# Seven-product down projection, paced between the gate and up products, in a SwiGLU encoder layer on one Trainium2 core

## The chip, the core and the metric

One NeuronCore of a Trainium2 chip runs the whole layer. Its engines work side by side, each through its own instruction queue in order: PE (TensorE, matrix products into PSUM), DVE (VectorE), ACT (ScalarE), POOL (GpSimd) and SP (SyncE, which here issues the loads and stores). The metric is the device time of one execution in microseconds (us), taken over several runs; less is better.

## What is computed

The layer works on 512 tokens of width 1024, in float32:

```
x  = LN1(alpha*x + 0.5*(silu(x@wg1) * (x@wu1)) @ wd1)      # FFN 1, wg/wu 1024x2816, wd 2816x1024
h  = x @ w_in ; sparse top-k attention (8 heads) and a gated short convolution on parts of h
x  = LN2(alpha*x + concat(attention, conv) @ w_out)
x  = LN3(alpha*x + 0.5*(silu(x@wg2) * (x@wu2)) @ wd2)      # FFN 2, same shapes
x  = x + sigmoid(x @ ple_gate_w) * (p @ ple_proj_w)
```

## The kernel before, in words

**Exactness.** Every float32 operand is kept as two tiles of TensorE's rounded format, `hi` and `lo` (their sum is the number), and every product is three matmuls: hi·hi, lo·hi and hi·lo in the order of `PASSES` (line 59). `split` (lines 110 to 112) makes the two: ACT casts `hi` (L111), DVE subtracts to get `lo` (L112). Tiles live in pages of 4 KB a partition, given out in a ring by `page` and `free` (lines 86 to 94); 38 of them.

**FFN.** `ffn` (from line 244) is called for both FFNs. The 2816 hidden columns are 22 chunks of 128. Chunks 0 and 1 are done by `plain` (L256 to L274). The others go in pairs by `two` (L309 to L352): a pair's gate and up products, 1024 x 256 weights against 1024 x 512 activations, are cut into quarters and done by seven products in place of eight (`prod`, L319). A product is 24 matmuls of 128x256 into a PSUM bank. ACT or DVE adds the seven results up in SBUF (L340 to L349): one ACT copy and seven DVE additions a pair. `weights` (L276 to L307) makes a pair's weight operands: per matrix four DVE sums and differences (L293, L294, L299, L300) and splits. `put_chunk` (L332) makes silu(gate)*up, and `put` splits it (L111, L112 with `hf`).

**Down projection.** The chunks are taken in groups of 4, 4, 4, 4 and 6 (`GROUPS1`, `GROUPS2`). After a group's chunks the down projection adds them to the output rows `nat`: for each half of the 1024 output columns and each of the four blocks of 128 tokens, every chunk's three 128x512 matmuls (L132) into one bank, and one DVE operation that scales and adds the bank to `nat` (L406). That is 2 x 4 x 4 x 3 = 96 matmuls and 8 of these additions for a group of four. `wd_rows` (L368) loads the weights 512 KB at a time and splits each (four for a group of four). The last group of six is also done so, with the layer norm behind it (L382 to L396).

**Order.** A scheduler puts the instructions on the engines by their place in the program, moved forward by the offsets of `tc.high_priority`; nothing else paces the operand work against PE.

Of the kernel before, what the change touches and what calls it, by code (L numbers as in the profile page):

```python
# [29 lines left out]
NPAGES = 38  # L30
WSTEPS = (1, 2, 1)
# [5 lines left out]
AHEAD_D2 = 0  # L37
NEMB = 2
# [25 lines left out]
def layer_kernel(ctx: ExitStack, tc: tile.TileContext, x, ln1_g, ln1_b, ffn1_wg, ffn1_wu, ffn1_wd, w_in,  # L64
# [3 lines left out]
    pp = ctx.enter_context(tc.tile_pool(name="pp", bufs=1, space=bass.MemoryType.PSUM))  # L68

# [22 lines left out]
    def free(*tiles):  # L92
        for t in tiles:
# [3 lines left out]
              "fill": BANKS[0], "qk": BANKS[1], "av": BANKS[2], "pt": BANKS[3]}  # L97
# [146 lines left out]
    def ffn(X, wg, wu, wd, ln_g, ln_b, first, load_nat, groups, nplain, ahead, ahead_f, ahead_d):  # L244
# [11 lines left out]
        def plain(fc, ws, cuts, ah):  # L256
# [13 lines left out]
            hf = ring("hf", 2, [P, 512])  # L270
            s_t = ring("a", 2, [P, 512])
            nc.scalar.activation(s_t, ps["g"], AF.Silu)
            nc.vector.tensor_mul(hf, s_t, ps["u"])
            return put(hf)  # L274

        def weights(w, fc, ops, pages):  # L276
# [8 lines left out]
            ops["A11"] = a11[:, 0], a11[:, 1]  # L285
            yield
            a2 = page([P, 4, 2 * P]), page([P, 4, 2 * P])
            split(*a2, r[1])
            ops["A12"], ops["A22"] = (tuple(z[:, :, m * P:(m + 1) * P] for z in a2) for m in range(2))
# [7 lines left out]
            ops["S1"], ops["S2"] = (tuple(z[:, i] for z in h12) for i in range(2))  # L297
            yield
            nc.vector.tensor_sub(S3, A11, A21)  # L299
            nc.vector.tensor_sub(S4, A12, S2)  # L300
            free(*r, s12)
# [4 lines left out]
            pages += [a11, *a2, *h12, *h34]  # L306
            yield  # L307

        def two(fc, ah):  # L309

            W, pages = {nm: {} for nm, _ in mats}, []
            steps = [weights(w, fc, W[nm], pages) for nm, w in mats]
            with tc.high_priority(offset=ah):
                for n in WSTEPS:
                    for g in steps:
                        for _ in range(n):
                            next(g)

            def prod(a, b):  # L319

                ps = bank("all").rearrange("p (m n) -> p m n", m=2)
                for i, (nm, _) in enumerate(mats):
                    mm(ps[:, i], [((W[nm][a][0][:, c], W[nm][a][1][:, c]), (X.q[b][0][:, c], X.q[b][1][:, c])) for c in range(4)])
                return ps


            e = [page([P, 2, 2, 256], F32) for _ in range(2)]
            k = [page([P, 2, 2, 256], F32) for _ in range(2)]
            p1, u2, u3, u4 = k[0][:, 0], k[0][:, 1], k[1][:, 0], k[1][:, 1]
            h = []  # L330

            def put_chunk(m):  # L332
                hf = ring("hf", 2, [P, 512])
                h3 = hf.rearrange("p (a b) -> p a b", a=2)
                s_t = ring("a", 2, [P, 2, 256])
                nc.scalar.activation(s_t, e[m][:, :, 0], AF.Silu)  # L336
                nc.vector.tensor_mul(h3, s_t, e[m][:, :, 1])  # L337
                h.append(put(hf))
# [4 lines left out]
            p5 = prod("S1", "T1")  # L343
            nc.vector.tensor_add(u4, p5, u2)
            nc.vector.tensor_add(e[0][:, 1], prod("S4", "B22"), u4)  # L345
            put_chunk(0)
            nc.vector.tensor_add(u3, prod("S3", "T3"), u2)
            nc.vector.tensor_add(e[1][:, 1], p5, u3)
            nc.vector.tensor_add(e[1][:, 0], prod("A22", "T4"), u3)  # L349
            put_chunk(1)  # L350
            free(*pages, *e, *k)
            return h  # L352

        f0 = 0
        for gi, per in enumerate(groups):
            last = gi == len(groups) - 1
            h = []
            while len(h) < per:
                fc = f0 + len(h)
                if fc < nplain:  # L360
                    h.append(plain(fc, first if fc == 0 else {}, 2, ahead))
                    if len(h) == nplain:
                        free(*X.q["B12"])
                        X.sums()
                else:
                    h += two(fc, ahead if fc < 4 else ahead_f)
            wds, held = {}, {}

            def wd_rows(i, half):
                if (i, half) not in wds:  # L370
                    n2 = min(2, per - i)
                    u = unit(rows(wd[:, half * 512:(half + 1) * 512], (f0 + i) * P, n2), [P, n2, 512], ahead_d)
                    for k in range(n2):
                        wds[i + k, half] = (u[0][:, k], u[1][:, k])
                        held[i + k, half] = u if k == n2 - 1 else ()
                return wds[i, half]

            if gi == 0 and load_nat:
                load_nat()
            if last:  # L380
                X.done()
                g_t, b_t = bcast(ln_g[0]), bcast(ln_b[0])  # L382
                yT = new_xT()
                for t in range(NTB):
                    for half in range(2):
                        acc = bank("all")
                        for i in range(per):
                            mm(acc, [(both(h[i], ts(t)), wd_rows(i, half))], first=i == 0, last=i == per - 1)
                            if t == NTB - 1:
                                free(*held[i, half])  # L390
                        dst = nat[t][:, half * 512:(half + 1) * 512]
                        nc.vector.scalar_tensor_tensor(dst, acc, CY, dst, op0=ALU.mult, op1=ALU.add)  # L392
                        nc.vector.bn_stats(stats[t][:, half], dst)
                    ln_tb(nat[t], stats[t], g_t, b_t)
                    transpose_tb(yT, t, "all")
            else:  # L396
                for half in range(2):
                    acc = [bank("all") for _ in range(NTB)]
                    for i in range(per):
                        wv = wd_rows(i, half)  # L400
                        for t in range(NTB):
                            mm(acc[t], [(both(h[i], ts(t)), wv)], first=i == 0, last=i == per - 1)
                        free(*held[i, half])
                    for t in range(NTB):
                        dst = nat[t][:, half * 512:(half + 1) * 512]
                        nc.vector.scalar_tensor_tensor(dst, acc[t], CY, dst, op0=ALU.mult, op1=ALU.add)  # L406
            free(*h)
            f0 += per
# [14 lines left out]
    def embed(t):  # L423

        prj.append(page([P, 1024], F32))
        for half in range(2):
            hs = slice(half * 512, (half + 1) * 512)
            ps = bank("fill" if t < NEMB else "all")
            mm(ps, [((p_T[0][:, c, ts(t)], p_T[1][:, c, ts(t)]),
                     (wp[c][0][:, 0, hs], wp[c][1][:, 0, hs])) for c in range(2)])  # L430
            nc.scalar.copy(prj[t][:, hs], ps)  # L431
            yield
# [3 lines left out]
    warm = sb.tile([P, 512], F32, name="warm")  # L436
# [110 lines left out]
    dm = sb.tile([P, 1280], F32, name="dm")  # L547
    for t in range(NTB):
        w_ = (t + 1) * P
        d = dm[:, TOFF[t]:TOFF[t + 1]]  # L550
# [4 lines left out]
    nc.vector.memset(dm[0:64, 64:128], -BIG)  # L555
# [18 lines left out]
    def choose():  # L574
# [105 lines left out]
    def softmax(h):  # L680
# [3 lines left out]
        a = soft[h] = ring("a", 2, [P, 1280])  # L684
        st = ring("ss", 2, [P, NTB, 3])
        for t in range(NTB):
            w_ = (t + 1) * P
            o = slice(TOFF[t], TOFF[t + 1])
            ps = bank("qk")
            mm64(ps[:, :w_], qT[j], e, ts(t), kT[j][:, e, :w_], kL[j][:, e, :w_])  # L690
            nc.vector.tensor_tensor_reduce(a[:, o], ps[:, :w_], dm[:, o], -slope, 3.0e38, ALU.add, ALU.min, st[:, t, 0:1])
            nc.scalar.activation(a[:, o], a[:, o], AF.Exp, bias=st[:, t, 0:1], scale=-1.0, accum_out=st[:, t, 1:2])
            nc.vector.reciprocal(st[:, t, 2:3], st[:, t, 1:2])
            nc.vector.tensor_scalar(a[:, o], a[:, o], st[:, t, 2:3], None, op0=ALU.mult)

# [46 lines left out]
    free(*v)  # L742
# [30 lines left out]
    for t in range(NTB):  # L773
# [39 lines left out]
```

## Time and profile before

| | |
|---|---|
| runs of the kernel before | 1024.43, 1026.31, 1027.77 us (median 1026.31) |
| the profiled execution | 1025.2 us, of which the span of its trace is 1023.2 us |
| busy over the span | PE 98%, DVE 80%, ACT 43%, POOL 2% |
| HBM traffic | 101 GB/s over the span |

The trace gives each instruction's engine, source line, tiles and time. The span runs from the first to the last instruction. A matmul's busy time is modelled and overlaps the next one's, so the pace of a stretch of matmuls is read from the starts of neighbouring stretches.

### The profile page before, as it was taken

How to read it: one execution, taken by the hardware profiler on the slowest of the kernel's cores; microseconds unless marked ns; L12 is line 12 of the kernel's file. 1: busy time of each engine (PE TensorE's matmuls, PEld its weight loads, DVE VectorE, ACT ScalarE, POOL GpSimd, SP SyncE). 2: the span in 40 equal slices, each digit the busy share in tenths (PEclk: the TensorE clock that was granted, in tenths of full speed). 3: DMA queues.
4: the chain of work that ended last, by engine and by line, in shares of the span. 5: the costliest groups of instructions: out<-in, count | busy, mean ns of one | idle time of the engine just before them, and what ended most of it. 6: DMA issues, size and time to landing. Idle time of an engine off the chain costs nothing.

```text
span 1023.2 us, 15533 instructions
## 1 busy us (share of the span) xinstructions
PE 1004.2 (98%) x6311; PEld 901.9 (88%) x6311; DVE 823.5 (80%) x1289; ACT 443.2 (43%) x627; POOL 25.0 (2%) x35
## 2 busy tenths in 40 slices
PE   8999999999999999999999999999999999999998
PEld 7989999898998878888878778989999898998887
DVE  7997868978697958999479988896868969689952
ACT  7444334433355235332586836543425325246221
POOL 1000000000000200000000011000000000000100
PEclk9999999999999999999999999999999999999999
DMA  9532324323245231514012222331324322227111
GB/s 303 159 114 81 107 83 145 94 80 115 83 138 183 62 95 36 143 37 124 21 53 92 83 76 90 131 117 47 119 84 145 102 80 88 82 90 260 53 41 51
DMA packets 99606, 104.57 MB, mean 102 GB/s; under 512 B 5968, under 2 KB 82000, under 8 KB 99536
## 3 DMA queue, kind: packets, MB, share of 16 engines
q1 hardware_dynamic: 99536, 103.60, 32.2%
q8 instruction: 49, 0.80, 0.3%
q14 instruction: 21, 0.17, 0.1%
HBM read 101.49 MB, written 2.10 MB: 101 GB/s over the span
## 4 chain that ended last, share of the span: by engine, by line
PE 89%; DMA 4%; DVE 3%; ACT 3%; SPq 1%; issue 1%; POOLq 0%; ACTq 0%; DVEq 0%
PE bk L132 85%; ACT pg L111 2%; DVE pg L112 1%; PE bk L522 1%; DMA pg<-in_ffn_wu_dram 1%; DMA pg<-in_w_in_dram 1%; PE bk L523 1%; PE bk L720 1%; DMA pg<-in_x_t_dram 1%; DMA pg<-in_ple_proj_w_dram 1%; DMA pg<-in_ffn_wd_dram 0%; SPq L214 0%; PE bk L146 0%; DMA pg<-in_ple_gate_w_dram 0%; PE bk L708 0%
## 5 line engine op out<-in xcount | busy, mean ns | idle before, releaser
L132 PE MATMUL bk<-pg,pg 128*128 128x256 f32 (+1 forms) x2832 | 496.0, 333 | 5.7 <-DVE nat L755 2.2
L132 PEld LDWEIGHTS bk<-pg,pg 128*128 128x128 f32 x2832 | 427.3, 190 | 57.4 <-ACT pg L111 3.1
L111 ACT CAST pg<-pg 128x1024 fp32r<-128x1024 f32 (+1 forms) x270 | 260.4, 976 | 309.9 <-PE bk L132 76.2
L112 DVE TENSOR_TENSOR pg<-pg,pg 128x1024 fp32r<-128x1024 f32 (+1 forms) x270 | 301.6, 1128 | 42.5 <-ACT pg L111 35.8
L132 PE MATMUL bk<-xq,pg 128*128 128x256 f32 x2208 | 274.4, 283 | 2.5 <-DVE mv L158 1.5
L132 PEld LDWEIGHTS bk<-xq,pg 128*128 128x128 f32 x2208 | 269.1, 192 | 6.5 <-ACT pg L431 1.9
L132 PE MATMUL bk<-xT,pg 128*128 128x512 f32 (+2 forms) x600 | 133.1, 381 | 0.3 <-ACT xT L111 0.2
L132 PEld LDWEIGHTS bk<-xT,pg 128*128 128x128 f32 (+1 forms) x600 | 109.9, 186 | 21.5 <-ACT xT L111 0.5
L132 PE MATMUL bk<-pg,xT 128*128 128x512 f32 (+1 forms) x312 | 69.5, 374 | 1.3 <-DVE nat L392 1.3
L132 PEld LDWEIGHTS bk<-pg,xT 128*128 128x128 f32 x312 | 55.0, 188 | 11.4 <-ACT pg L111 1.7
L336 ACT ACTIVATE a<-pg 128x512 f32<-128x512 f32 x40 | 25.2, 631 | 70.3 <-DVE pg L345 63.6
L111 ACT CAST pg<-hf 128x512 fp32r<-128x512 f32 (+1 forms) x56 | 34.6, 619 | 38.6 <-DVE hf L337 20.8
L112 DVE TENSOR_TENSOR pg<-hf,pg 128x512 fp32r<-128x512 f32 (+1 forms) x56 | 38.4, 685 | 4.3 <-ACT pg L111 4.0
L406 DVE SCALAR_TENSOR_TENSOR nat<-bk,nat 128x512 f32<-128x512 f32 x64 | 40.4, 683 | 0.5 <-PE bk L132 0.2
L337 DVE TENSOR_TENSOR hf<-a,pg 128x512 f32<-128x512 f32 x40 | 27.5, 688 | 14.5 <-ACT a L336 14.5
L345 DVE TENSOR_TENSOR pg<-bk,pg 128x512 f32<-128x512 f32 x20 | 13.8, 691 | 27.8 <-PE bk L132 27.5
L160 POOL TENSOR_TENSOR mv<-mv,mhalf 128x1 f32<-128x1 f32 x12 | 17.8, 1481 | 628.0 <-DVE mv L159 628.0
L293 DVE TENSOR_TENSOR pg<-pg,pg 128x512 f32<-128x512 f32 x40 | 27.2, 686 | 5.9 <-DMA pg<-in_ffn_wg_dram 5.9
L299 DVE TENSOR_TENSOR pg<-pg 128x512 f32<-128x512 f32 x40 | 27.5, 686 | 3.0 <-PE bk L132 3.0
L112 DVE TENSOR_TENSOR pg<-bk,pg 128x512 fp32r<-128x512 f32 (+2 forms) x37 | 22.5, 627 | 8.5 <-ACT pg L111 8.1
L294 DVE TENSOR_TENSOR pg<-pg,pg 128x512 f32<-128x512 f32 x40 | 27.3, 684 | 0.0
L300 DVE TENSOR_TENSOR pg<-pg,pg 128x512 f32<-128x512 f32 x40 | 27.1, 685 | 0.1
(100 smaller groups left out, 613.8 us busy)
## 6 DMA issues: line engine op xcount, KB each, us to landing
pg<-in_ffn_wd_dram SPq DMA_DIRECT2D x44, 512.0 KB, 4.0
pg<-in_ffn_wu_dram SPq DMA_DIRECT2D x43, 512.0 KB, 4.7
pg<-in_ffn_wg_dram SPq DMA_DIRECT2D x43, 512.0 KB, 3.9
pg<-in_w_in_dram SPq DMA_DIRECT2D x28, 512.0 KB, 3.6
pg<-in_w_out_dram SPq DMA_DIRECT2D x8, 512.0 KB, 3.9
pg<-in_ple_gate_w_dram SPq DMA_DIRECT2D x8, 512.0 KB, 5.1
pg<-in_x_t_dram SPq DMA_DIRECT2D x8, 256.0 KB, 5.9
nat<-in_x_dram SPq DMA_DIRECT2D x4, 512.0 KB, 9.2
```

Of the source, the lines that this page charges most:

```text
L111: nc.scalar.copy(hi, src)
L112: nc.vector.tensor_sub(lo, src, hi.bitcast(F32))
L132: nc.tensor.matmul(ps, lhsT=st[a], rhs=mv[b], start=first and i == 0 and k == 0, stop=last and i == n - 1 and k == 2)
L160: nc.gpsimd.tensor_tensor(mv[:, 3:4], mv[:, 2:3], mhalf, op=ALU.pow)
L293: nc.vector.tensor_add(S1, A21, A22)
L294: nc.vector.tensor_sub(S2, S1, A11)
L299: nc.vector.tensor_sub(S3, A11, A21)
L300: nc.vector.tensor_sub(S4, A12, S2)
L336: nc.scalar.activation(s_t, e[m][:, :, 0], AF.Silu)
L337: nc.vector.tensor_mul(h3, s_t, e[m][:, :, 1])
L345: nc.vector.tensor_add(e[0][:, 1], prod("S4", "B22"), u4)
L406: nc.vector.scalar_tensor_tensor(dst, acc[t], CY, dst, op0=ALU.mult, op1=ALU.add)
```

## The change

In both FFNs the down projection of the first four groups is done by the same seven-product scheme as the pairs. A group of four chunks is two pairs; token halves, the two chunks of a pair and the two halves of the output columns are the quarters. A product is 12 matmuls of 128x512: two banks (token blocks), two pairs, three passes. The results are not added up in SBUF: a bank holds a running sum of products, and after a product DVE adds the bank to each part of `nat` that contains that sum.

The products' operands: `pair_ops` makes the hidden side (one split of 768 columns, four DVE sums of 256, one split of 1024 a pair). `Down.prep` makes the weight side: four DVE differences (L305), and for each of the seven operands `parts`: ACT writes minus the rounded weight into `lo` (L299), a DMA issued by POOL adds the weight to `lo` in SBUF (L300), ACT casts `hi` (L301). The seven splits' DVE subtraction is thus not there.

The pairs' own products add up in PSUM in the same way, with four ACT copies and three DVE additions a pair. Their banks are four, the down projection's the other four. One list, `order`, fixes which product follows which: from the third product of the next pair on, two down products after three pair products. Loads and operand work stand in the program at a set planned time ahead of their product. Chunks 0 and 1 and the last group of six stay as they were.

There are 41 pages now. The embedding product `prj` goes to DRAM after it is made and is loaded again at the end; the attention's `dm` and softmax rows are in pages.

```diff
-NPAGES = 38
-WSTEPS = (1, 2, 1)
+NPAGES = 41
+LEAD_L, LEAD_S, LEAD_DL, LEAD_DS = 16.0, 8.0, 18.0, 13.0
+T_PLAIN, T_PAIR, T_DOWN = 11.5, 2.9, 2.7
...
+        def pair_ops(pair):
+            A12, A22, A11, A21 = (pair[:, i] for i in range(4))
+            a = page([P, 4, 256]), page([P, 4, 256])
+            split(a[0][:, :3], a[1][:, :3], pair[:, :3])
+            s_ = page([P, 4, 256], F32)
+            nc.vector.tensor_add(s_[:, 0], A21, A22)
...
+            split(*sums, s_)
...
+            def parts(self, name):
+                src = self.raw[name]
+                hi, lo = self.w[name] = page([P, 2, 512]), page([P, 2, 512])
+                nc.scalar.mul(lo, src, -1.0)
+                nc.gpsimd.dma_start(lo, src, accum_op=ALU.add)
+                nc.scalar.copy(hi, src)
...
+            def product(self, banks, a, w, first, *outs):
+                w = self.w.pop(w)
+                for b in range(2):
+                    for i, (q, sums) in enumerate(self.pairs):
+                        st = sums if a[0] == "S" else q
+                        for n, (x_, y_) in enumerate(PASSES):
+                            nc.tensor.matmul(banks[b], lhsT=st[x_][:, SLOT[a], ts(b)], rhs=w[y_][:, i],
+                                             start=first and i == 0 and n == 0, stop=i == 1 and n == 2,
+                                             skip_group_check=not first)
+                free(*w)
+                for m, n in outs:
+                    for b in range(2):
+                        dst = nat[2 * m + b][:, n * 512:(n + 1) * 512]
+                        nc.vector.scalar_tensor_tensor(dst, banks[b], CY, dst, op0=ALU.mult, op1=ALU.add)
+            def products(self):
+                two_banks = lambda: [bank("down") for _ in range(2)]
+                x_, y_ = two_banks(), two_banks()
+                self.product(x_, "A11", "B11", True, (0, 0))
+                yield
+                self.product(y_, "S1", "T1", True, (1, 1))
+                yield
+                self.product(x_, "S2", "T2", False, (0, 1))
+                yield
+                self.product(x_, "S3", "T3", False, (1, 1))
+                yield
+                self.product(y_, "S4", "B22", False, (0, 1))
...
+                self.product(x_, "A22", "T4", False, (1, 0))
+                yield
+                self.product(two_banks(), "A12", "B21", True, (0, 0))
...
-            nc.scalar.copy(p1, prod("A11", "B11"))
-            nc.vector.tensor_add(e[0][:, 0], prod("A12", "B21"), p1)
-            nc.vector.tensor_add(u2, prod("S2", "T2"), p1)
...
+                nc.scalar.copy(e[0][:, 0], product(x_, "A11", "B11", True))
+                yield
+                nc.scalar.copy(e[1][:, 1], product(y_, "S1", "T1", True))
+                yield
+                nc.scalar.copy(e[0][:, 1], product(x_, "S2", "T2", False))
+                yield
+                nc.vector.tensor_add(e[0][:, 1], product(y_, "S4", "B22", False), e[0][:, 1])
+                yield
+                nc.vector.tensor_add(e[1][:, 1], product(x_, "S3", "T3", False), e[1][:, 1])
+                yield
+                nc.vector.tensor_add(e[0][:, 0], product(bank2(), "A12", "B21", True), e[0][:, 0])
+                self.put_chunk(0, e[0])
+                yield
+                nc.scalar.copy(e[1][:, 0], product(x_, "A22", "T4", False))
+                self.put_chunk(1, e[1])
+                yield
...
+            for i, _ in enumerate(chain_pairs(pairs)):
+                if i >= 2 and i % 3 != 1:
+                    next(downs, None)
...
+        for i, (us, f) in enumerate(order):
+            while todo and todo[0][0] <= max(at[i], 0.0):
+                t_, _, g_ = todo.pop(0)
...
+            f()
...
+                nc.sync.dma_start(prj[t], pr)
...
+        with tc.high_priority(offset=AHEAD_G):
+            nc.sync.dma_start(pr, prj[t])
```

PE before, at the start of the first group's down projection (`bk` are PSUM banks, first operand the hidden side, second the weights' first 512 columns; the four banks are the four token blocks):

```order
359 L132 MATMUL bk_631<-pg_57_637,pg_12_236 128x512 [waits PE_49]
360 L132 MATMUL bk_631<-pg_58_638,pg_12_236 128x512
361 L132 MATMUL bk_631<-pg_57_637,pg_12_236 128x512
362 L132 MATMUL bk_632<-pg_57_637,pg_12_236 128x512 [waits Activation_49]
363 L132 MATMUL bk_632<-pg_58_638,pg_12_236 128x512
364 L132 MATMUL bk_632<-pg_57_637,pg_12_236 128x512
```

Ninety-six such matmuls stand in one block there, after the group's last pair.

PE in the changed kernel, at the sixth down product (A22·T4) of the second group in FFN 1. L444 are pair products, L339 down products; `pg_206` and `pg_207` are T4's `hi` and `lo`, and the wait on DMASW4 is on the DMA that finishes `lo`:

```order
1054 L444 MATMUL bk_1678<-pg_21_356,pg_204_1654 128x256
1055 L339 MATMUL bk_1431<-pg_206_1673,pg_110_973 128x512 [waits Activation_49]
1056 L339 MATMUL bk_1432<-pg_206_1673,pg_110_973 128x512 [waits DVE_49]
1057 L444 MATMUL bk_1679<-xq_0_77,pg_210_1748 128x256 [waits Activation_49]
1058 L444 MATMUL bk_1679<-xq_0_78,pg_210_1748 128x256
1059 L444 MATMUL bk_1892<-xq_0_77,pg_220_1835 128x256
...
1065 L444 MATMUL bk_1678<-pg_23_361,pg_210_1748 128x256 [waits Activation_49]
1066 L339 MATMUL bk_1431<-pg_207_1674,pg_110_973 128x512 [waits DMASW4_49]
1067 L339 MATMUL bk_1431<-pg_206_1673,pg_111_974 128x512
```

Two matmuls with T4's `hi` and nine of pair products stand ahead of the first one with `lo`; before them come a whole pair product (`bk_1678`, 24 matmuls, its last is row 1054) and a whole down product (12 matmuls), and before that the pair product into `bk_1679`.

ACT at the same place (L466 and L468 copy the banks of the pair's first two products, L301 and L299 make T4's `hi` and the start of its `lo`; `pg_205` is T4):

```order
117 L466 COPY pg_208_1680<-bk_1678 128x512 [waits PE_49]
118 L115 CAST pg_195_1637<-pg_194_1632 128x1024 [waits DVE_49]
119 L468 COPY pg_209_1681<-bk_1679 128x512 [waits PE_49]
120 L301 CAST pg_206_1673<-pg_205_1671 128x1024 [waits DVE_49,Activation_49]
121 L115 CAST pg_210_1748<-pg_198_1642 128x1024
122 L299 ACTIVATE pg_207_1674<-pg_205_1671 128x1024 [waits DVE_49]
123 L299 ACTIVATE pg_215_1759<-pg_191_1598 128x1024 [waits DMAHW1_49,DMASW3_49,PE_49]
```

T4's `lo` is begun only after the copy that waits for the product into `bk_1679` and two casts. The same order stands in six of the eight groups, in the first three of each FFN.

## Rows read from the trace of the kernel before

**Rows 1.** The page: span, busy us of each engine, granted PE clock.

```profile
span 1023.2 us, 15533 instructions
...
PE 1004.2 (98%) x6311; PEld 901.9 (88%) x6311; DVE 823.5 (80%) x1289; ACT 443.2 (43%) x627; POOL 25.0 (2%) x35
...
PEclk9999999999999999999999999999999999999999
```

**Rows 2.** The chain of waits: start us, us, what; its longest pieces.

```profile
14.91 302.68 PE bk L132 x2177
...
628.62 305.82 PE bk L132 x2201
...
981.70 37.31 PE bk L132 x187
```

**Rows 3.** The timeline of PE, FFN 1: start us, us, engine, line, operation.

```profile
59.79 13.99 PE L132 MATMUL bk<-pg,pg 128*128 128x512 f32 x61
73.61 5.92 PE L132 MATMUL bk<-xq,pg 128*128 128x256 f32 x48
79.37 3.04 PE L132 MATMUL bk<-pg,pg 128*128 128x256 f32 x24
```

**Rows 4.** Windows over three periods of FFN 1: busy us (x count).

```profile
73.61:135.71 62.10, 62.10 (x433) 58.34 (x432) 50.63 (x69) 25.51 (x31) 0.00 (x0) 1.00 0.32 102
135.71:197.81 62.10, 62.10 (x433) 58.34 (x432) 49.70 (x67) 24.64 (x30) 0.00 (x0) 1.00 0.32 102
197.81:259.91 62.10, 62.10 (x433) 58.34 (x432) 49.74 (x67) 24.76 (x30) 0.00 (x0) 1.00 0.32 103
```

**Rows 5.** Groups by line and form: busy us, mean ns | idle before.

```profile
L112 DVE TENSOR_TENSOR pg<-pg,pg 128x1024 fp32r<-128x1024 f32 x223 | 270.2, 1222 | 38.3 <-ACT pg L111 32.2 <-PE bk L132 2.9 <-ACT a L336 2.7
...
L111 ACT CAST pg<-pg 128x1024 fp32r<-128x1024 f32 x223 | 232.6, 1051 | 268.7 <-PE bk L132 62.1 <-DVE pg L294 52.7 <-DMA pg<-in_ffn_wd_dram 46.3
...
L406 DVE SCALAR_TENSOR_TENSOR nat<-bk,nat 128x512 f32<-128x512 f32 x64 | 40.4, 683 | 0.5 <-PE bk L132 0.2
...
L294 DVE TENSOR_TENSOR pg<-pg,pg 128x512 f32<-128x512 f32 x40 | 27.3, 684 | 0.0
...
L340 ACT COPY pg<-bk 128x512 f32<-128x512 f32 x20 | 11.7, 586 | 15.8 <-PE bk L132 14.9 <-DVE pg L112 0.9
...
L112 DVE TENSOR_TENSOR pg<-bk,pg 128x256 fp32r<-128x256 f32 x8 | 3.3, 415 | 0.0
```

**Rows 6.** The timeline of DVE in FFN 1; in brackets idle time and releaser.

```profile
134.57 2.48 DVE L406 SCALAR_TENSOR_TENSOR nat<-bk,nat 128x512 f32<-128x512 f32 x4
...
165.32 2.35 DVE L112 TENSOR_TENSOR pg<-pg,pg 128x1024 fp32r<-128x1024 f32 x2
...
170.47 0.69 DVE L345 TENSOR_TENSOR pg<-bk,pg 128x512 f32<-128x512 f32 x1 [2.19 <-PE bk L132]
```

**Rows 7.** DMA issues: tensor, queue, count, KB each, median us to landing.

```profile
pg<-in_ffn_wd_dram SPq DMA_DIRECT2D x44, 512.0 KB, 4.0
...
pg<-in_ple_gate_w_dram SPq DMA_DIRECT2D x8, 512.0 KB, 5.1
...
nat<-in_x_dram SPq DMA_DIRECT2D x4, 512.0 KB, 9.2
```

**Rows 8.** Waits: engine, line, for whom: us in total, times, longest us.

```profile
ACT pg L111 <- DVE pg L294: 52.7, 25, 4.3
DVE pg L112 <- ACT pg L111: 47.9, 59, 3.3
```

**Rows 9.** Group by line: the only operation of POOL that repeats.

```profile
L160 POOL TENSOR_TENSOR mv<-mv,mhalf 128x1 f32<-128x1 f32 x12 | 17.8, 1481 | 628.0 <-DVE mv L159 628.0
```

More of the change, by code (lines that the diff above doesn't have):

```diff
@@ L284, in weights @@
             split(a11[:, 0], a11[:, 1], A11)
[L285 to L289, printed above, removed]
+            ops["A11"] = (a11[:, 0], a11[:, 1]), [a11]
             yield
@@ L305, in weights @@
             ops["S3"], ops["S4"] = (tuple(z[:, i] for z in h34) for i in range(2))
[L306 removed]
+            ops["S3"], ops["S4"] = (ops["S3"], h34), (ops["S4"], [])
             yield
[L309 to L321, printed above, removed]
[L322 to L352 removed]
@@ L354, in ffn @@
[L354 to L364, printed above, removed]
-                else:
[L366 to L402, printed above, removed]
-                        free(*held[i, half])
[L404 to L408, printed above, removed]
@@ new lines, in ffn, with add_pair @@
+        order, begin = [], []
+        def add_pair(fc, place, done):
+            u = Two(fc, place)
+            prods = u.products()
+            uses = {0: [(LEAD_L, u.prep), (LEAD_S, u.prep)], 1: [(LEAD_S, u.prep)], 3: [(LEAD_S, u.prep)], 5: [(LEAD_S, u.prep)]}
+            for i in range(7):
+                for lead, f in uses.get(i, ()):
+                    begin.append((lead, len(order), f))
+                order.append((T_PAIR, (lambda: next(prods)) if i < 6 else (lambda: (next(prods), done()))))
+                yield
@@ new lines, in add_down @@
+        def add_down(f0, pairs):
+            u = Down(f0, pairs)
+            prods = u.products()
+            loads = {0: ((0, 0),), 1: ((0, 1),), 2: ((1, 1),), 5: ((1, 0),)}
+            for i in range(7):
+                for at in loads.get(i, ()):
+                    begin.append((LEAD_DL, len(order), lambda at=at: u.load(*at)))
+                begin.append((LEAD_DS, len(order), lambda i=i: u.prep(i)))
+                order.append((T_DOWN, lambda: next(prods)))
+                yield
@@ new lines, in ffn, with place_in, first_chunks @@
+        per = groups[-1]
+        n_down = (len(groups) - 1)
+        ops = [[] for _ in range(n_down)]
+        pair_of = {}
+        def place_in(n, m):
+            if n not in pair_of:
+                pair_of[n] = page([P, 4, 256], F32)
+            return raw_of(pair_of[n], m)
+        def first_chunks():
+            for m in range(2):
+                plain(m, first if m == 0 else {}, 2, ahead, place_in(0, m))
+            free(*X.q["B12"])
+            X.sums()
+            ops[0].append(pair_ops(pair_of[0]))
@@ new lines, in ffn, with late_place, late_done, chain_pairs @@
+        order.append((2 * T_PLAIN, first_chunks))
+        h = []
+        late = {}
+        def late_place(n, m):
+            late[n, m] = ring("hf", 2, [P, 2, 256])
+            return late[n, m]
+        def late_done(n):
+            for m in range(2):
+                h.append(put(late[n, m].rearrange("p a b -> p (a b)")))
+        def chain_pairs(pairs):
+            for n in pairs:
+                if n < 2 * n_down:
+                    yield from add_pair(2 * n, lambda m, n=n: place_in(n, m), lambda n=n: ops[n // 2].append(pair_ops(pair_of[n])))
+                else:
+                    yield from add_pair(2 * n, lambda m, n=n: late_place(n, m), lambda n=n: late_done(n))
@@ new lines, in ffn @@
+        for _ in chain_pairs((1,)):
+            pass
+        if load_nat:
+            order.append((0.0, load_nat))
+        for g in range(n_down):
+            pairs = (2 * g + 2, 2 * g + 3) if g < n_down - 1 else (2 * g + 2, 2 * g + 3, 2 * g + 4)
+            downs = add_down(4 * g, ops[g])
+            for i, _ in enumerate(chain_pairs(pairs)):
+                if i >= 2 and i % 3 != 1:
+                    next(downs, None)
+            for _ in downs:
+                pass
+        at = [0.0]
@@ new lines, in ffn, with wd_rows @@
+        f0 = 4 * n_down
+        wds, held = {}, {}
+        def wd_rows(i, half):
+            if (i, half) not in wds:
+                n2 = min(2, per - i)
+                u = unit(rows(wd[:, half * 512:(half + 1) * 512], (f0 + i) * P, n2), [P, n2, 512], ahead_d)
+                for k in range(n2):
+                    wds[i + k, half] = (u[0][:, k], u[1][:, k])
+                    held[i + k, half] = u if k == n2 - 1 else ()
+            return wds[i, half]
+        X.done()
+        g_t, b_t = bcast(ln_g[0]), bcast(ln_b[0])
@@ new lines, in ffn @@
+        yT = new_xT()
+        for t in range(NTB):
+            for half in range(2):
+                acc = bank("all")
+                for i in range(per):
+                    mm(acc, [(both(h[i], ts(t)), wd_rows(i, half))], first=i == 0, last=i == per - 1)
+                    if t == NTB - 1:
+                        free(*held[i, half])
+                dst = nat[t][:, half * 512:(half + 1) * 512]
+                nc.vector.scalar_tensor_tensor(dst, acc, CY, dst, op0=ALU.mult, op1=ALU.add)
+                nc.vector.bn_stats(stats[t][:, half], dst)
+            ln_tb(nat[t], stats[t], g_t, b_t)
+            transpose_tb(yT, t, "all")
@@ L409, in ffn @@
+        free(*h)
         free(g_t, b_t)
@@ L423, in embed @@
     def embed(t):
-        prj.append(page([P, 1024], F32))
+        pr = page([P, 1024], F32)
         for half in range(2):
```

145 lines of the change are left out of this document (122 added, 23 removed).

## Prediction

> **What bounds the kernel now.** I read the page first. PE is busy for 1004.2 of the span's 1023.2 us and the granted clock is at its full level in all forty slices [rows 1]. The reader should see that DVE (823.5 us) and ACT (443.2 us) are well below. The chain of waits says the same: FFN 1 and FFN 2 are two unbroken pieces of 302.68 and 305.82 us of matmuls [rows 2]. So inside the FFNs a matmul that goes is time that goes, and a matmul that waits is time that comes.
>
> The price of a matmul is the pace between starts in the timeline of PE: 61 matmuls of 128x512 take 73.61 - 59.79 = 13.82 us, 0.227 us each, and 48 of 128x256 take 5.76 us, 0.120 us each [rows 3]. Three windows of one period each (two pairs and a group's down projection) show 62.10 us of PE in each [rows 4]. The prices rebuild it: 14 products of 24 at 0.120 and 96 at 0.227 are 40.3 + 21.8 = 62.1 us. In the same period DVE is busy 50 us and ACT 25 us, and DMA 0.32 of the time [rows 4].
>
> **The change, part by part.**
>
> *Fewer matmuls.* A group's down projection goes from 96 to 7 x 12 = 84 matmuls of the same form. That is 12 x 0.227 = 2.72 us a group, and 21.8 us for the eight groups of both FFNs. The matmuls stand on PE's unbroken chain [rows 2], so all of it counts. The period becomes 59.4 us.
>
> *DVE.* By the program a period has 66 operations now, 50 of 512 columns and 16 of 1024. By the groups' means, 0.684 and 1.222 us [rows 5], they sum to 53.8 us; the window shows 50 us busy [rows 4], 0.93 of it, since neighbours overlap: four L406 take 2.48 us and two L112 2.35 us [rows 6]. The changed period has 72: 18 of 1024, 44 of 512 (14 of them adding banks to `nat`, L346, like L406), two of 768 (0.93 each by width) and eight of 256 (0.415 [rows 5]). They sum to 22.0 + 30.1 + 1.9 + 3.3 = 57.3 us, and 0.93 of that is 53.3 of 59.4 us. DVE's idle time falls from 12.1 to 6.1 us a period. Its cover is PE: the banks are four and four, and a bank read after a pair product is wanted again one or more products (2.7 us each) later, against a read of 0.68 us. Cost 0; if that cover goes, the second rival is what follows.
>
> *ACT.* A period has 16 casts of 1024 columns and 14 operations of 512 now: at 1.051 and about 0.6 us [rows 5] 25.2 us, as the window shows [rows 4]. Afterwards it is 28 of 1024 (14 of them L299 and L301), two of 768 and 16 of 512, 40.7 us of 59.4 us. No ACT multiplication of 1024 columns is in the trace; I give it a cast's 1.051 us. There is room, but ACT's order matters now, since PE waits behind it (below).
>
> *The accumulating DMA.* Each of the 56 weight operands gets its `lo` from a DMA that POOL issues, 512 KB from SBUF to SBUF. The trace of before has no such transfer. Nearest rows: a 512 KB load of `wd` lands in a median of 4.0 us, `gate_w` in 5.1, `x` in 9.2 [rows 7]; POOL's only repeated operation takes 1.48 us on a single column [rows 9], so POOL isn't prompt. Below, nothing excludes a quicker one than 4.0, as no HBM is touched. I take 5.1: the accumulation reads two streams where `wd` reads one, and POOL makes the issue, but it doesn't meet the start-up crowd that the `x` loads do.
>
> *Where that DMA counts.* For six of the seven operands the order of the program leaves 14 us or more of PE work between ACT's multiplication and the first matmul with `lo`: cost 0. The sixth, T4, is different in the first three groups of each FFN, as the order of ACT and PE shows. ACT begins T4's `lo` only after the copy (L468) that waits for the pair's second product, a cast L301, a cast L115 and then L299: 0.586 + 3 x 1.051 = 3.74 us [rows 5] after that product has ended. From there PE has a down product (12 x 0.227 = 2.72), a pair product (24 x 0.120 = 2.88), two down matmuls (0.45) and nine pair matmuls (1.08) before the first matmul with `lo`: 7.13 us. So 7.13 - 3.74 = 3.4 us are left for the DMA. At 5.1 us PE waits 1.7 us, six times: 10.2 us. Queued behind that wait are the rest of the product and the next pair product, and on DVE the `lo` of the pair's S3 and S4, which waits for the same page; the ten remaining down matmuls (2.27 us) cover DVE's 1.22 us for it.
>
> *The rest.* `prj` goes to DRAM and back by four stores and four loads on SP's queue: hidden behind the attention and the final gate products; without that cover one 5.1 us load [rows 7] at most. The loads of the FFN stand 16 to 18 us of planned time ahead against a landing of 4 to 5 us [rows 7]: 0. At an FFN's start S1 is now the second operand wanted and its DVE sums stand early in the weights' chain; the waits between ACT's cast and DVE's sum are 4.3 us at the longest [rows 8], so 0 to 4 us per FFN; I take 0, as the plain chunks (23 us of PE) run ahead of it. Attention pages: 0.
>
> *Sum.* Against the profiled execution of 1025.2 us: 1025.2 - 21.8 + 10.2 = 1013.6 us. The median of the runs is 1.1 us above that execution, so the forecast is **1014.5 us** (1014.7 rounded down to the half).
>
> **Weighed against the skill.** The measured loads took 4.0 us and more for 512 KB [rows 7]. The Trainium skill, "DMA: Bandwidth & Descriptors", section "Anatomy of one DMA — SWDGE (gpsimd) path", fits a DMA issued by GpSimd as 2.0 us plus its bytes at 436 GB/s; my estimate from that page is 3.2 us for 512 KB, by which T4 would never be waited for and the time would be about 1004.5; no run here shows such a DMA, and its fit isn't of an accumulating one. Against the change speaks "SBUF — State Buffer", section "Who interferes with whom" (the Trainium skill): a DVE instruction with two SBUF inputs contends with a GpSimd instruction that reads SBUF, and a DMA issued by GpSimd can be starved of port time; most of DVE's operations here have two SBUF inputs. Whether issuing is hit no row shows.
>
> **The rivals.**
>
> *Whole gain.* The DMA takes up to 4.4 us, or PE's slack elsewhere takes the wait: at most 1 us is lost at six places. The `wd` row's 4.0 us [rows 7] speaks for it. 1026.3 - 21.8 = 1004.5 us, up to 1010.
>
> *Slow accumulation (the other side).* One mechanism, at T4: the DMA takes 6.2 us or more. The gain is eaten when it takes 3.4 + 21.8 / 6 = 7.0 us; at the 9.2 us of the `x` loads [rows 7] PE waits 5.8 us six times, 34.8 us, and the time is 1004.5 + 34.8 = 1039 us. For it: reading, adding and writing in one transfer, an issue by an engine that takes 1.48 us for one column [rows 9], and other loads on the same DMA engines (0.32 of them busy [rows 4]). Against: 9.2 us was seen only where all first loads fall together.
>
> *DVE becomes the bound.* Its idle 12.1 us a period now are partly waits for ACT and PE (59 waits for L111, 3.3 us at the longest [rows 8]). If all of them stayed, the period would be 53.3 + 12.1 = 65.4 us in place of 62.1, 1026 + 8 x 3.3 = 1052 us; it is slower from 8.8 us of waits on. Against: the idle time stands where DVE waits for PE's products (2.19 us before L345 [rows 6]), and a later DVE finds those done.
>
> *The change doesn't do what it says.* The order of PE has exactly 96 matmuls fewer in the FFNs, so I give that nothing.
>
> **How the numbers follow.** About 0.3% (3.1 us) is what a measurement can tell from no change: 1023.2 to 1029.4 us. Forecast, DMA of 4.4 to 6.2 us at T4 or waits of that size elsewhere: 1010 to 1021, chance 0.42. Whole gain: 0.25. Slow accumulation, 1021 to 1040: 0.20 (0.04 faster, 0.08 the same, 0.08 slower). DVE the bound, 1030 to 1052: 0.08, slower. Something not listed, such as the FFNs' starts or the pages' turn: 0.05 (0.01 the same, 0.04 slower). So faster 0.71, the same 0.09, slower 0.20. The range goes from 1002.5 (the whole gain and the 1.9 us by which the fastest run lies under the median) to 1034 (a T4 wait of 5 us); above it are most of the DVE case, a part of the slow accumulation and of the rest, under 0.15. The forecast's own range is 1010 to 1021.
>
> **What the profile after would show.** Right: 84 matmuls L339 a group, a period of 59.4 us without and 61.1 us with a wait, six waits of PE at L339 for a DMA of about 1.7 us each, accumulating DMAs of about 5 us, DVE near 53 us and ACT near 40 us a period, clock full. Wrong: PE idle at L444 or at a bank (then DVE or the order of operands is late, not the DMA), waits at other products than T4, or no wait at all with a period still above 60 us.

## The result and the profile after

The changed kernel takes 1073.06 us (median of four runs, 1072.53 to 1077.54) against 1026.47 us of the kernel before on the same chip: a ratio of 1.0465, with a 95% interval of 1.0432 to 1.0499. It was forecast at 1014.5 us, in a range of 1002.5 to 1034. The profiled execution has a span of 1070.4 us.

The page of the changed kernel, the lines that answer to [rows 1]:

```profile
span 1070.4 us, 15655 instructions
...
PE 1003.4 (94%) x6215; PEld 896.3 (84%) x6215; DVE 838.8 (78%) x1321; ACT 550.7 (51%) x767; POOL 74.9 (7%) x91
...
PEclk9998998999999999999999999998998999999999
```

PE has 96 matmuls fewer (6215 against 6311), and yet is busy as long as before: part of the rest ran at a lower clock. Two slices in each FFN show 8 tenths. The waits, by engine, line and releaser (us in total, times, longest us):

```profile
DVE pg L116 <- DMA pg<-pg: 41.5, 7, 7.1
PE bk L339 <- DMA pg<-pg: 40.4, 6, 7.1
```

PE waits six times at a down product (L339) for an accumulating DMA, 40.4 us in all. DVE waits for the same DMA. The timeline of PE at the first of the six places (start us, us, line; idle time and releaser in brackets), which answers to [rows 3]:

```profile
89.16 2.91 PE L339 MATMUL bk<-pg,pg 128*128 128x512 f32 x12
91.90 3.04 PE L444 MATMUL bk<-pg,pg 128*128 128x256 f32 x24
94.78 0.63 PE L339 MATMUL bk<-pg,pg 128*128 128x512 f32 x2
95.25 1.10 PE L444 MATMUL bk<-xq,pg 128*128 128x256 f32 x8
96.18 0.37 PE L444 MATMUL bk<-pg,pg 128*128 128x256 f32 x1
103.37 4.56 PE L339 MATMUL bk<-pg,pg 128*128 128x512 f32 x10 [6.82 <-DMA pg<-pg]
107.77 2.80 PE L444 MATMUL bk<-xq,pg 128*128 128x256 f32 x22
```

This is T4's product: two matmuls with `hi`, nine of pair products, then the wait for `lo`. The ten matmuls behind it take 4.40 us from their first start to the next block's (107.77 - 103.37), 0.44 each where 0.227 is the full pace [rows 3]. ACT and POOL at that place:

```profile
89.36 0.59 ACT L468 COPY pg<-bk 128x512 f32<-128x512 f32 x1 [0.30 <-PE bk L444]
89.84 1.05 ACT L301 CAST pg<-pg 128x1024 fp32r<-128x1024 f32 x1
90.80 1.05 ACT L115 CAST pg<-pg 128x1024 fp32r<-128x1024 f32 x1
91.74 2.00 ACT L299 ACTIVATE pg<-pg 128x1024 fp32r<-128x1024 f32 x2
```

```profile
93.16 1.81 POOL L300 DMA_DIRECT2D pg<-pg  x2 [16.22 <-ACT pg L299]
```

ACT's copy starts when the pair's second product has ended, the two casts follow, then L299 for T4 and, without a gap, L299 for B21. POOL issues both DMAs back to back. In the chain of waits T4's DMA takes 10.17 us:

```profile
93.16 10.17 DMA pg<-pg
103.33 0.04 issue
103.37 4.56 PE bk L339 x10
```

SP's queue shows what else was on its way:

```profile
91.19 0.92 SPq L394 DMA_DIRECT2D pg<-in_ffn_wg_dram  x2
92.20 1.01 SPq L394 DMA_DIRECT2D pg<-in_ffn_wu_dram  x2
93.31 0.58 SPq L293 DMA_DIRECT2D pg<-in_ffn_wd_dram  x1
```

Five loads of 512 KB in some 2.7 us. The windows of the wait, of the ten matmuls and of what follows (us, then busy us of PE, PEld, DVE, ACT, POOL with counts, the granted clock, DMA share, GB/s) show the 16 DMA engines full during the wait, and the clock at 0.52 of full speed, close to the lower level (1.2 of 2.4 GHz), in the ten matmuls:

```profile
96.55:103.37 6.82, 0.00 (x1) 0.00 (x1) 0.02 (x1) 0.08 (x1) 0.00 (x0) 0.82 1.03 238
103.37:107.93 4.56, 4.56 (x12) 3.63 (x13) 2.50 (x3) 1.66 (x2) 0.00 (x0) 0.52 0.59 170
107.93:140.51 32.58, 32.58 (x240) 30.96 (x239) 28.44 (x38) 19.19 (x23) 3.48 (x4) 1.00 0.62 156
```

From one such wait to the next is a period, to be read against [rows 4]:

```profile
103.37:171.90 68.53, 62.03 (x421) 57.69 (x421) 52.55 (x73) 37.61 (x46) 6.09 (x7) 0.95 0.58 144
171.90:239.97 68.07, 61.90 (x421) 57.59 (x421) 52.62 (x73) 37.71 (x46) 6.08 (x7) 0.95 0.57 142
```

**Where the time went**, in spans (1023.2 to 1070.4, +47.2 us):

| | us |
|---|---|
| 96 matmuls fewer | -21.8 |
| six waits of PE for T4's `lo` (6.82, 6.50, 6.17, 7.13, 6.77, 7.06) | +40.5 |
| the ten matmuls behind each at the lower clock: 26.9 us in place of 60 x 0.227 = 13.6 | +13.3 |
| ends of the FFNs: waits for bank copies in the last pair (FFN 1 3.7 and 1.5 of clock behind, FFN 2 2.9) | +8.1 |
| first layer norm, first to last transposes (26.9 to 31.0) | +4.1 |
| from there to the second layer norm's transposes (243.1 to 247.0), and these (19.5 to 16.6) | +1.0 |
| not assigned | +2.0 |

The 26.9 us are the lengths of the six blocks, in which the tail of the last matmul counts. From start to start the six take 25.9 us, so some 12.2 of the 13.3 us are the lower clock.

### The profile page after: what moved, and what is told of

It is laid out like the page before. It is cut to its first block, busy times and chain, and to the rows that moved or that the text cites. A ratio compares the mean times of both kernels' runs of the same rounds, so it can differ in the third digit from the quotient of the medians.

```text
span 1070.4 us, 15655 instructions
## 1 busy us (share of the span) xinstructions
PE 1003.4 (94%) x6215; PEld 896.3 (84%) x6215; DVE 838.8 (78%) x1321; ACT 550.7 (51%) x767; POOL 74.9 (7%) x91
## 4 chain that ended last, share of the span: by engine, by line
PE 50%; issue 24%; DMA 12%; DVE 8%; ACT 3%; POOL 2%; SPq 0%; POOLq 0%; DVEq 0%; ACTq 0%
PE bk L136 24%; PE bk L444 16%; PE bk L339 7%; DMA pg<-pg 6%; DVE pg L116 3%; DMA pg<-in_ffn_wg_dram 2%; ACT pg L115 2%; DMA pg<-in_ffn_wd_dram 2%; POOL pg L300 2%; DMA pg<-in_w_out_dram 1%; DVE nat L166 1%; PE bk L716 1%; POOL mv L164 1%; PE bk L150 1%; PE bk L717 1%
## 5 line engine op out<-in xcount | busy, mean ns | idle before, releaser
L115 ACT CAST pg<-pg 128x1024 fp32r<-128x1024 f32 (+2 forms) x270 | 254.3, 962 | 236.1 <-DVE pg L116 56.9
L116 DVE TENSOR_TENSOR pg<-pg,pg 128x1024 fp32r<-128x1024 f32 (+2 forms) x270 | 294.8, 1112 | 94.3 <-ACT pg L115 50.7
L444 PE MATMUL bk<-xq,pg 128*128 128x256 f32 x1920 | 244.8, 285 | 5.9 <-ACT pg L479 3.4
L444 PEld LDWEIGHTS bk<-xq,pg 128*128 128x128 f32 x1920 | 240.3, 193 | 11.3 <-ACT pg L479 3.8
L339 PE MATMUL bk<-pg,pg 128*128 128x512 f32 x672 | 176.3, 412 | 40.4 <-DMA pg<-pg 40.4
L339 PEld LDWEIGHTS bk<-pg,pg 128*128 128x128 f32 x672 | 130.1, 201 | 66.9 <-DMA pg<-pg 41.6
L444 PE MATMUL bk<-pg,pg 128*128 128x256 f32 x1440 | 184.1, 283 | 1.1 <-ACT pg L466 1.1
L444 PEld LDWEIGHTS bk<-pg,pg 128*128 128x128 f32 x1440 | 178.9, 192 | 3.6 <-ACT pg L466 1.5
L136 PE MATMUL bk<-pg,pg 128*128 128x512 f32 (+1 forms) x624 | 141.8, 378 | 3.5 <-DVE pg L116 1.7
L346 DVE SCALAR_TENSOR_TENSOR nat<-bk,nat 128x512 f32<-128x512 f32 x112 | 76.6, 687 | 20.5 <-PE bk L339 19.6
L300 POOL DMA_DIRECT2D pg<-pg x56 | 49.2, 878 | 536.7 <-ACT pg L299 336.0
L301 ACT CAST pg<-pg 128x1024 fp32r<-128x1024 f32 x56 | 58.3, 1045 | 33.8 <-PE bk L444 28.4
L299 ACT ACTIVATE pg<-pg 128x1024 fp32r<-128x1024 f32 x56 | 58.6, 1058 | 14.1 <-DVE pg L305 14.1
L305 DVE TENSOR_TENSOR pg<-pg,pg 128x1024 f32<-128x1024 f32 x32 | 39.0, 1218 | 1.6 <-PE bk L444 1.5
```

The source lines that it names most:

```text
L115: nc.scalar.copy(hi, src)
L116: nc.vector.tensor_sub(lo, src, hi.bitcast(F32))
L136: nc.tensor.matmul(ps, lhsT=st[a], rhs=mv[b], start=first and i == 0 and k == 0, stop=last and i == n - 1 and k == 2)
L299: nc.scalar.mul(lo, src, -1.0)
L300: nc.gpsimd.dma_start(lo, src, accum_op=ALU.add)
L301: nc.scalar.copy(hi, src)
```

## The experiments

**Theory A:** T4's accumulating DMA lands late because it shares the DMA engines with SP's five loads and with B21's accumulation; the lower clock comes behind the wait. **Rivals:** DVE has no room and T4's `lo` is late however it is made; it is the number of accumulating DMAs; the wait only moves on. Times are medians; each run is compared with the kernel before on the same chip (1025.76 to 1028.13 us).

### T4 by DVE: `t4_dve`

```diff
+                if name in ('T4',):
+                    split(hi, lo, src)
+                    return
                 nc.scalar.mul(lo, src, -1.0)
                 nc.gpsimd.dma_start(lo, src, accum_op=ALU.add)
```

> T4's lo by a DVE subtraction, no DMA. Theory A (the accumulating DMA of T4, crowded by other transfers, is the wait; TensorE's half clock comes after that wait): the six waits at L339 (40.5 us) and the six half-clock stretches behind them (13.3 us) go, about 1019 us (1016 to 1024). Rival B (DVE is full there, so T4's lo is late in any case): waits of 1 to 2 us stay at the six places, 1028 to 1038 us. Rival C (the wait only moves to B21's DMA, issued beside it): 1045 us or more.

Measured: 1033.51 us, ratio 1.0057 (1.0038 to 1.0076). The six waits are gone, and 39.6 us of the 54 expected. The time lies in rival B's range, but none of the waits that it names is there. In their place PE waits for ACT's copies of the banks (L469, L471 and L482), 9.5 + 6.7 + 3.8 = 20.0 us in many short waits. The waits of ACT and the timelines of ACT and PE show how that comes:

```profile
ACT pg L115 <- DMA pg<-pg: 32.2, 5, 6.7
```

```profile
102.66 1.14 ACT L115 CAST pg<-pg 128x512 fp32r<-128x512 f32 x2 [6.46 <-DMA pg<-pg]
```

```profile
114.99 3.13 PE L447 MATMUL bk<-xq,pg 128*128 128x256 f32 x24 [0.80 <-ACT pg L482]
119.29 2.89 PE L447 MATMUL bk<-pg,pg 128*128 128x256 f32 x22 [1.18 <-ACT pg L469]
```

ACT stands for 6.46 us behind B21's DMA, still in the burst, for a page (five such waits, 32.2 us in all). In the chain of waits that delay goes on to DVE's operations, for some 13 us, and from them to ACT's copy at L469, which PE waits for. So a form of rival C held for a part: the wait moved to other engines.

### B21 by DVE: `b21_dve`

The same edit for B21 alone.

> B21's lo by a DVE subtraction, T4's still by DMA: T4's DMA has no second accumulation beside it. If the second accumulation is what doubles it: it lands in about 5.7 us, waits of 2.2 us, 1035 to 1045 us. If the five loads that SP issues within 3 us of it are: it lands in 8.5 us or more, waits of 5 us or more, 1060 to 1073 us.

Measured: 1064.77 us, ratio 1.0365 (1.0333 to 1.0397). T4's DMA is now POOL's only one there, and still takes 8.89 to 10.50 us (mean 9.67) against 9.47 to 10.43 (mean 10.05) in the change:

```profile
93.24 8.89 DMA pg<-pg
...
160.63 10.11 DMA pg<-pg
```

The second accumulation accounts for little; the loads are left.

### T4 begun earlier: `t4_17`

```diff
-                begin.append((LEAD_DS, len(order), lambda i=i: u.prep(i)))
+                begin.append(({5: 17.0}.get(i, LEAD_DS), len(order), lambda i=i: u.prep(i)))
```

> T4's operand begun 17 instead of 13 us of planned time ahead; everything else as in the change. Theory A: its DMA is issued some 4 us earlier, waits of 2 to 3 us stay, 1035 to 1050 us; less if it comes ahead of the burst of loads. Rival D (pages: what T4 takes earlier is missing for the loads, and another operand is late): no better than 1065 us.

Measured: 1079.5 us, ratio 1.0496 (1.0454 to 1.0538): no better. PE waits only 0.4 us for an accumulating DMA now, but other waits took that place, as rival D has it:

```profile
PE bk L339 <- DVE nat L346: 18.0, 10, 3.8
...
SPq L293 <- DVE pg L410: 122.2, 4, 33.6
...
DVE pg L305 <- DMA pg<-pg: 15.6, 3, 5.7
...
DVE pg L403 <- DMA pg<-pg: 12.1, 2, 6.4
```

SP stands up to 33.6 us for a page before a `wd` load. DVE stands 27.7 us, in five waits, for pages that accumulating DMAs still hold, and reaches the additions to `nat` late. In a ring of 41 pages the earlier start seems to take a page from another operand. That it is the number of pages is argued from these waits: no run had more.

### No accumulating DMA: `all_dve`

The edit of `t4_dve` for all seven operands.

> All seven lo by DVE subtractions, no accumulating DMA at all. DVE's sum for a period is 57.3 + 7 x 1.22 = 65.8 us, 0.93 of it 61.2 us, over the 59.4 us of PE: DVE becomes the bound, period 61 to 63 us, 1030 to 1048 us. If DVE has slack that this sum misses: about 1015 to 1020 us.

Measured: 1013.31 us, ratio 0.9867 (0.9837 to 0.9897), 1.3% faster than the kernel before. The page, and windows from one group's first down product to the next group's (columns as in the windows above):

```profile
PE 989.5 (98%) x6215; PEld 885.3 (87%) x6215; DVE 895.6 (89%) x1377; ACT 503.1 (50%) x711; POOL 25.8 (3%) x35
```

```profile
60.48:120.64 60.16, 59.90 (x422) 56.14 (x421) 59.20 (x79) 30.85 (x39) 0.00 (x0) 1.00 0.34 106
120.64:180.56 59.92, 59.84 (x422) 55.83 (x421) 59.02 (x79) 31.20 (x39) 0.00 (x0) 1.00 0.34 106
```

The period is 60.2 and 59.9 us against 59.4 from the matmuls alone and 62.1 before [rows 4]. DVE's 79 operations take 59.1 us of it, where my sum had 61.2 and DVE as the bound: that missed, and the other branch, slack that the sum didn't see, came, a little under its 1015 us. DVE is all but full, and the seven subtractions just fit. The rival of a DVE without room falls.

### T4 alone by DMA: `t4_only`

The edit for the other six.

> Only T4's lo by the accumulating DMA, the other six by DVE. Theory A (T4's DMA among the burst of five loads is what costs): its DMA lands in 8 to 9 us, six waits of 5 to 6 us with half-clock stretches behind, 1013 + 6 x 7.5 = 1055 us (1048 to 1065). Rival (it is the number of accumulating DMAs, 56 of them): 1013 to 1020 us.

Measured: 1063.73 us, ratio 1.0359 (1.0335 to 1.0383). Against `all_dve` that is 50 us more by eight DMAs of 56. Six of them are waited for at length, 35.0 us (a seventh for 0.58), and the ten matmuls behind the six take 13.0 us too long: 48.0 us. (The sum in the expectation, 1013 + 6 x 7.5, is 1058 and not 1055.) T4's DMA among five loads is enough for the loss, and the number of accumulating DMAs is not the cause.

### T4 and B21 by DVE: `t4b21_dve`

> T4 and B21 by DVE, the other five by the accumulating DMA. If what was left over in the run with T4 alone by DVE is ACT standing 6.5 us behind B21's DMA (a page of it) and then being late with the banks' copies: 1012 to 1018 us. If it is ACT's sum of work (the multiplications L299): 1025 us or more.

Measured: 1015.35 us, ratio 0.9895 (0.9876 to 0.9914). ACT's wait for an accumulating DMA isn't among its waits any more, and PE's waits for its copies (L469, L471) fall to 3.8 us. The multiplications L299 of the other five are still on ACT: it wasn't the sum of its work. Five of seven operands by DMA cost next to nothing where the two in the burst are not.

### Loads later: `loads10` and `t4_only10`

```diff
-LEAD_L, LEAD_S, LEAD_DL, LEAD_DS = 16.0, 8.0, 18.0, 13.0
+LEAD_L, LEAD_S, LEAD_DL, LEAD_DS = 10.0, 8.0, 18.0, 13.0
```

`loads10` has it on the change, `t4_only10` on `t4_only`.

> All seven by the accumulating DMA as in the change; the pairs' weight loads take their pages 10 instead of 16 us of planned time ahead, so they come later. If the burst of loads is what slows T4's DMA: it lands in 5.5 to 7 us, waits of 2 to 3.5 us, 1030 to 1050 us. If accumulating DMAs are slow for themselves there: 1065 us or more. Against it stands that a load may then itself be late.

> Only T4's lo by the accumulating DMA, and the pairs' loads 10 instead of 16 us ahead: the fourth corner beside the change (two accumulating DMAs, early loads: 10.2 us to landing), t4_only (one, early loads: 9.0) and loads10 (two, late loads: 6.9). If loads cost 2 to 3 us of the landing and the second accumulation 1 to 2: it lands in 5 to 6 us, six waits of 1.5 to 2.5 us, 1013 + 6 x (2 + 2) = 1037 us (1025 to 1042). If the late loads helped loads10 in another way: 1050 us or more.

`loads10`: 1051.09 us, ratio 1.0252 (1.0222 to 1.0282), 1 us above the range. All seven operands by DMA, B21's beside T4's, and T4's lands in 6.55 to 6.85 us, as expected if the burst is what slows it. The loads that SP issues within 3 us of it are two in place of five. The second `wu` load of the row below is issued only at 101.89 us, when T4's DMA has landed (the row's 8.46 us span both):

```profile
90.81 0.37 SPq L293 DMA_DIRECT2D pg<-in_ffn_wd_dram  x1
93.79 8.46 SPq L394 DMA_DIRECT2D pg<-in_ffn_wu_dram  x2
```

```profile
93.71 6.85 DMA pg<-pg
...
159.47 6.77 DMA pg<-pg
```

`t4_only10`: 1057.04 us, ratio 1.0287 (1.0252 to 1.0322). My 1037 missed, and the time lies in the other branch's range. With other pages free the loads of FFN 1 moved elsewhere than in `loads10`: four came within 3 us of T4's DMA, most of them behind it, and it took 7.12 to 8.69 us there.

```profile
93.86 0.93 SPq L397 DMA_DIRECT2D pg<-in_ffn_wg_dram  x2
95.62 0.37 SPq L397 DMA_DIRECT2D pg<-in_ffn_wu_dram  x1
96.09 0.86 SPq L293 DMA_DIRECT2D pg<-in_ffn_wd_dram  x1
```

```profile
93.94 8.69 DMA pg<-pg
```

In FFN 2 two loads stand there, 2.9 us ahead of T4's DMA and 0.1 us behind its issue, as in `loads10` (the second `wu` load of the row comes at 738.47):

```profile
727.51 0.37 SPq L293 DMA_DIRECT2D pg<-in_ffn_wd_dram  x1
730.49 8.35 SPq L397 DMA_DIRECT2D pg<-in_ffn_wu_dram  x2
```

```profile
730.41 6.74 DMA pg<-pg
```

So FFN 2 is the fourth corner that I wanted: the same two loads, no second accumulation, and 6.74 to 6.98 us against 6.55 to 6.85 with it. The 5 to 6 us that I expected missed there too, since I had given the second accumulation 1 to 2 us and it costs nothing. In the last group of FFN 2 no load is issued within 3 us of T4's DMA (the next comes at 922.09), and it lands in 4.5 us. PE doesn't wait for it. The row gives tensor, queue, count, size and the time to landing, here of that one DMA (918.79 us):

```profile
pg<-pg POOLq DMA_DIRECT2D x1, 512.0 KB, 4.5
```

| run | loads within 3 us of T4's DMA | second accumulation | T4's DMA, mean, us | waits, us | lost behind them (block lengths), us |
|---|---|---|---|---|---|
| changed kernel, six places | 5 | yes | 10.05 | 40.5 | 13.3 |
| `b21_dve`, six places | 5 | no | 9.67 | 37.2 | 13.4 |
| `t4_only`, six places | 5 | no | 9.2 | 35.0 | 13.0 |
| `t4_only10`, FFN 1, three places | 4 | no | 7.9 | 14.1 | 6.1 |
| `t4_only10`, FFN 2, three places | 2 | no | 6.86 | 10.2 | 6.1 |
| `loads10`, six places | 2 | yes | 6.71 | 19.7 | 11.9 |

The 56 accumulating DMAs of the changed kernel say the same. Nine of them met no load in flight, seven of these another accumulation, and took 4.5 to 5.4 us. Nineteen met five loads in flight and took 6.1 to 12.5 us. So the landing follows the loads. Of theory A, B21's accumulation falls: it adds 0.4 to 0.9 us by the first three rows and nothing by the last two. No run is without a load near T4's DMA at the six places.

### The mask out of the layer norm: `all_dve_dm`, `all_dve_late`, and two beside it

In the changed kernel `dm` lies in pages, so its operations on POOL and DVE (L750 to L752 in `all_dve`) start only when pages are free, in the first layer norm. `all_dve_dm` gives `dm` its own tile and leaves 40 pages; `all_dve_late` writes these operations after the attention's score products. `t4b21_late` and `all_dve_late12` (loads 12 us ahead) do the latter too.

> All seven by DVE, and the attention's dm in a tile of its own again (40 pages). If the mask's operations (L750 to L752 in the profile) that stood in the layer norm's chain cost the 4 us there: 1008 to 1011 us. If not, or if a page fewer costs as much: 1013 us or more.

> All seven by DVE, 41 pages, and the mask's operations written after the attention's score products, so that they don't stand in the first layer norm's chain. If they cost the 4 us there (as the run with dm in a tile of its own has it between the first and last transposes: 27.2 against 30.8 us): 1008 to 1011 us. If the layer norm only passes the wait on: 1013 us or more.

> T4 and B21 by DVE, the other five by the accumulating DMA, the mask's operations moved as in the run beside it. 1010 to 1013 us if the two effects add up; DMA against DVE for those five is then worth 0 to 2 us either way.

> As the first of this call, with the pairs' loads taking pages 12 instead of 16 us ahead. Without accumulating DMAs a burst of loads holds nobody up: within 3 us of the first. If the loads then come late: slower by 5 us or more.

`all_dve_dm`: 1025.06 us, ratio 0.9992 (0.9975 to 1.001). The layer norm is back at 27.2 us, but FFN 1 reaches its transposes 4.1 us later and FFN 2 takes some 5 us more: a page fewer cost more than the mask.

`all_dve_late`: 1011.85 us, ratio 0.9850 (0.9834 to 0.9866), the lowest median of all, and between the two branches of its expectation. The wait before the last transposes, in `all_dve` and then in `all_dve_late`:

```profile
361.58 1.97 PE L150 MATMUL bk<-ident,nat 128*128 128x128 f32 x8 [4.02 <-DVE nat L166]
```

```profile
359.15 1.09 PE L150 MATMUL bk<-ident,nat 128*128 128x128 f32 x8 [1.97 <-DVE nat L166]
```

The stretch is 28.7 us in place of 30.8. Over the whole kernel 1.5 us lie between the two, and their intervals overlap; that the move helps the total isn't shown. `t4b21_late` has 1013.6 us (0.9850 to 0.9895) and `all_dve_late12` 1012.24 us (0.9841 to 0.9874), both the same within their intervals. Without the accumulating DMAs, loads that come 12 in place of 16 us ahead cost nothing.

## Why the prediction was wrong

- **What bounds the kernel, and the gain.** Right. Inside the FFNs the 96 matmuls are worth what was said: with T4 and B21 off the DMA the period is 59.5 to 60.2 us against the forecast 59.4.
- **The place and the order there.** Right. 3.74 us were forecast from the product's end to T4's DMA: from ACT's copy at 89.36 us to POOL's issue at 93.16 it is 3.80. The DMA was to have 3.4 us before PE comes to `lo`: PE stops at 96.55, 3.39 us after the issue. It is six places, at T4, with DVE's `lo` behind it. PE waits for no other operand's DMA, though B21's takes 11.5 to 12.5 us.
- **The DMA's price: the step that failed.** "It doesn't meet the start-up crowd that the `x` loads do", and so 5.1 us. It does meet one: five loads within 3 us of it, and 10.05 us in the mean, above even my upper end of 9.2. The six waits are 40.5 us in place of 10.2. By the break-even that the prediction names, 7.0 us, the change had to lose; the rival of a slow accumulation was the case, and had 0.20. What makes the DMA slow is the loads beside it, which that rival names last, and not the accumulation: 4.5 us with no load near (`t4_only10`). Its price of 1039 us was too low, too. The break-even was too high: `loads10` lands T4's DMA in 6.71 us and is still 2.5% slower than before.
- **The clock.** Not in the sum at all, 13.3 us with the tails, and "clock full" stood among the signs of being right. A wait on PE was priced at its length; it cost some 2 us more in each of the six places, whether the wait was 3.1 us (`loads10`) or 7.1 us (here).
- **"The rest" at 0.** Some 15 us: 8.1 for the last pairs' waits for bank copies, which I didn't name, 4.1 in the first layer norm, and 3 elsewhere or not assigned. The layer norm falls under "Attention pages: 0", a term put at nothing without a reason: with `dm` out of the pages its stretch is back at 27.2 us (`all_dve_dm`).
- **DVE and ACT.** DVE is busy 52.6 us a period (forecast 53.3), ACT 37.7 (near 40); neither is the bound. The DVE rival is refuted by `all_dve`, where DVE has seven operations more a period, 59 us of work in 60, and PE hardly waits.
- **The Trainium skill's rules.** The shortest accumulating DMA took 4.5 us, the median 5.7 (512 KB), so the 3.2 us, an estimate worked out from the Trainium skill ("DMA: Bandwidth & Descriptors", "Anatomy of one DMA — SWDGE (gpsimd) path"), is below every one here. Starved issues aren't seen: POOL's 56 issues take 0.86 to 1.04 us. The prediction read the Trainium skill too broadly there: the section it names, "Who interferes with whom" of "SBUF — State Buffer", says that a `tensor_tensor` was not seen to stall a DMA. What bears on this case is a section of the Trainium skill's "DMA: Bandwidth & Descriptors", "Issuing engines are not separate DMA queues": DMAs run on the same 16 engines and interleave, whichever engine started them. POOL's DMA among SP's loads agrees with it, 10.05 us against 4.5.

## What to carry to other kernels

Price a transfer by what else is in flight at the place where it is waited for, not by the median of its kind; read the other queues' order for the same microseconds. An operation that leaves a busy vector engine for a DMA gains nothing while that engine still has room, and takes on a latency that other queues set. A wait on TensorE costs its length and, where the clock falls, a stretch at half pace behind it.

## What the runs showed of the hardware

- A DMA issued by POOL that adds 512 KB to a tile in SBUF landed in 4.5 us with no load within 3 us, 6.6 to 7.0 beside two loads of 512 KB, 7.1 to 8.7 beside four and 7.3 to 10.6 beside five (`t4_only10`, `loads10`, `b21_dve`, `t4_only`, the changed kernel). A second such DMA made no difference beside two loads (6.71 us in the mean with it, 6.86 without).
- Behind waits of 3.1 to 7.1 us in five runs, the next ten matmuls of 128x512 took 4.0 to 4.6 us in place of 2.27, nearly the same after short and long ones. Behind PE's waits of 0.8 and 1.18 us in `t4_dve` the matmuls of 128x256 kept the full pace. In between it went either way: behind a wait of 1.96 us at the end of FFN 1 in the changed kernel 24 matmuls of 128x256 took 4.62 us at a granted clock of 0.63, and behind one of 2.04 us in `t4_only10` the clock stayed full.
- An engine that isn't waited for can pass a DMA's delay on: ACT, at half load, stood 32.2 us in five waits for pages, and PE waited 20.0 us for its copies, in short waits (`t4_dve`; 3.8 us in `t4b21_dve`).
- DVE can be busy for 59.2 of 60.16 us with PE at 59.90 (`all_dve`): two engines that hand each other banks and operands all the time were both full.

The two waits of about 2 us, in the changed kernel and in `t4_only10`:

```profile
322.18 4.62 PE L444 MATMUL bk<-xq,pg 128*128 128x256 f32 x24 [1.96 <-ACT pg L479]
```

```profile
297.42 2.79 PE L342 MATMUL bk<-pg,pg 128*128 128x512 f32 x11 [2.04 <-DMA pg<-pg]
```
